# Gate and up projections: hi and lo of the tokens in one matmul of 512 columns

## The chip, the cores and the metric

One core of one Trainium2 chip runs the whole program. The metric is the device time of one execution in microseconds (us): the median of three runs. All numbers of where the time goes come from one profiled execution of the same kernel, whose times are counted from the first instruction.

## What is computed

Three decoder layers on 256 tokens of 1024 features, in f32. Each has a mixer (a first kind in layer 1, another in layers 2 and 3), an out-projection, and a feed-forward part. The change is in the feed-forward part, which is the same in all three layers:

```python
h = rms_norm(x, gain)                                   # [256, 1024]
f = (jax.nn.silu(h @ w_gate) * (h @ w_up)) @ w_down     # 1024 -> 2816 -> 1024
x = x + f                                               # in layer 1: x + rms_norm(f, gain)
```

## The kernel before, in words

**Hi and lo.** Products run in fp32r. For precision each side of a product is a pair: hi, the value rounded to fp32r, and lo, what is left. `h @ w` is made of three products: hi by hi, lo by hi, hi by lo. A weight tile of 128 x 1024 (512 KB) comes by one DMA into `wraw` (3 buffers, `raw_weight`, L267 to L270). `split` (L276 to L284) makes `whi` from it on ScalarE (ACT, L279) and `wlo` on VectorE (DVE, L281); each has 5 buffers. `wraw` is free again when L281 is done, and then the next DMA can start, so the three `wraw` buffers go round in a ring: DMA, ACT, DVE, DMA.

**The feed-forward part** (`ffn`, L528 to L602) walks over 22 tiles `f` of 128 hidden features. Tiles 0 and 1 are made with tokens on partitions, ahead of the loop (L556 to L575). The loop (L577 to L595) takes f = 2 to 21. For each `f`, gate and up are made one after the other by `fm` (L427 to L433), with features on partitions and all 256 tokens as the columns that pass the array: for each of the 8 k-tiles three matmuls of 256 columns, L431 (`whi` by hi of the tokens), L432 (`whi` by lo of the tokens), L433 (`wlo` by hi of the tokens). That is 48 matmuls of 256 columns for each `f`. Gate fills the first half of a PSUM bank and up the second; even tiles use a bank of tag `p`, odd ones of tag `r`, two banks each.

The bank is then read: ACT makes silu of the gate half (L583), DVE multiplies it by the up half (L584), ACT makes hi of the hidden tile (L586) and DVE lo (L587). The tiles `sl` and `hd` share 10 buffers of one tag. The hidden tile passes the down projection (`flush`, `down`, `rows`, `mm3`: L313 to L315, matmuls of 512 columns into the banks `s`, `t`, `o`) one turn later, behind gate and up of the next `f`.

The last six tiles (NLATE) go into the result of tokens 0 to 127 in the loop, and into that of tokens 128 to 255 only behind it (L599 to L601), so that the next norm can begin on the first half of the tokens. Their down weights are split into space of the mixers (`weight_to`, L291 and L292), with no need of a `whi` buffer. The weights of the next layer's in-projection follow in the same ring of `wraw`.

**The tokens.** `put_T` (L382) writes hi (ACT, L389) and lo (DVE, L390) of the normed rows into two tiles, `hTh` and `hTl`, each 8 k-tiles by 256 tokens. The latent attention of layers 2 and 3 uses their space again (`room`, L1394).

**The order of the work.** Each engine runs its instructions in order, in the order that the framework's scheduler gives them when the program is built, by its own estimate of durations; it starts from the order of the program text. So an ACT or DVE instruction that waits for a matmul holds back what stands behind it on its engine, the splits of weights among them.

Of the kernel before, what the change touches and what calls it, by code (L numbers as in the profile page):

```python
# [10 lines left out]
F32 = mybir.dt.float32  # L11
F32R = mybir.dt.float32r
# [6 lines left out]
S = 256  # L19
# [8 lines left out]
# columns of "pcol" (parameters that go with features on partitions)  # L28
# [15 lines left out]
# rows of "prow" (parameters that are spread over all partitions)  # L44
# [11 lines left out]
# constants: the arrays they come in, name and number of columns  # L56
# [8 lines left out]
# Slots of a tag are given out in order: streams that run side by side have tags of their own.  # L65
# [6 lines left out]
class Names:  # L72
    """what the parts of a mixer share"""


# the order in which the steps of a layer's mixers are laid down. Layer 1: (b)ias, (p)rojections, attention of
# the first (m) and the last (n) heads, linear (r)ecurrence, (g)ated linear attention. Layers 2 and 3: (i)nverses,
# (v)alues, (o)perands and outp(u)ts of the recurrence, the rest of the (c)ompressed inputs, (d)ilated and (l)atent attention.
PLAN1 = "pprpbbrppmmpgbmgpmgrgbgprprggngngppngnr"
PLAN2 = "iciiiiiididlilliviiliiiolloodooilioidooidiilolodouullioouuuouluu"  # L80
# the order of the feature tiles in the out-projections
# [12 lines left out]
def _consts():  # L94
# [29 lines left out]
    # column j is distance j - 127  # L124
# [12 lines left out]
def _tm(k, *cols):  # L137
    return [(i, i + k, *cols) for i in range(0, KC, k)]


def _fm(*starts):
# [3 lines left out]
# weight tiles [128, k-tiles, columns] of the in-projections, in the order of their use  # L145
G1 = (_tm(2, 2320, 2576, 768, 1024) + _fm(1296, 1424, 1808, 1936)   # mv of four heads | gv, mq, mk of four heads
      + _fm(0, 128, 512, 640) + _tm(2, 2576, 2832, 1024, 1040)      # lru_x, gq, gk, mv | g_lr
      + _fm(1552, 1680, 2064, 2192) + _tm(4, 1040, 1296)            # mq, mk, g_out
      + _fm(256, 384))                                              # lru_g
G2 = (_tm(2, 1824, 2272, 1024, 1056) + _tm(4, 1568, 1824)              # cq | ckv | krope | lora input, dilated v  # L150
      + _fm(768, 896, 256, 384, 0, 128, 512, 640)                      # lora inputs, k, r, v
      + _tm(2, 1056, 1568))                                            # dilated q | k
# [16 lines left out]
def _pack_ffn(gate, up, down):  # L169
    g = np.asarray(gate).reshape(KC, 128, FC, 128)  # L170
    u = np.asarray(up).reshape(KC, 128, FC, 128)
    d = np.asarray(down).reshape(FC, 128, D)
    # the first two tiles of features: k-tiles in pairs, columns (gate | up)
    h = np.stack([g[:, :, :2], u[:, :, :2]], 2).reshape(4, 2, 128, 512).transpose(0, 2, 1, 3).reshape(4, 128, 1024)
    g, u = (v.transpose(2, 1, 0, 3).reshape(FC, 128, 1024) for v in (g, u))
    rest = np.stack([g[2:], u[2:], d[2:]], 1).reshape(-1, 128, 1024)
    return np.ascontiguousarray(np.concatenate([h, d[:2], rest], 0))
# [6 lines left out]
def layout(i):  # L184
    """The arrays of the launch: the inputs, laid out anew."""
# [46 lines left out]
def tile_kernel(ctx: ExitStack, tc: tile.TileContext, a: dict, out: bass.AP, taps: dict = {}):  # L232
# [33 lines left out]
    # ---------------------------------------------------------------- weights  # L266
# [5 lines left out]
    def weight(ap, E=None):  # L272
        """the pair (hi, lo) whose sum is ap [128, n]"""
        return split(raw_weight(ap), E)
# [11 lines left out]
    def weight_to(ap, his, los):  # L286
        """the same, in tiles that are given: lists of pieces along the columns"""
# [23 lines left out]
    def mm3(o, xs, ws, start, stop):  # L311
        """o += x^T w for the pairs (hi, lo) of both sides, but for lo times lo."""
# [4 lines left out]
    # ---------------------------------------------------------------- start  # L317
# [38 lines left out]
    # ---------------------------------------------------------------- norms  # L356
    @contextmanager
    def behind(done):
        """what is laid down inside is issued after the instructions done"""
# [12 lines left out]
    def mean_rstd(src0, src1, eps_n=1.0 / 32):  # L372
        """1 / rms of the rows [src0, src1] of 2 x 512 columns"""
# [8 lines left out]
    def put_T(src, n, dst, k0, t, tag):  # L382
        """n blocks [128 tokens, 128] of src to dst (hi, lo)[:, k0 + i, tokens of tile t]"""
# [9 lines left out]
    def norm(t, g, add=None, late=False):  # L393
        """the normed rows of tile t, in halves; add(h) first makes half h of x; late: g comes late"""
# [19 lines left out]
    def rows_T(xs, t, dst, tags="rr"):  # L414
        """features on partitions"""
# [10 lines left out]

    def fm(wt, hT, o):  # L427
        """128 features (the columns of the tile wt), all tokens: o [128, 256]"""
# [6 lines left out]
    def tm(wts, hT, t, o):  # L435
        """tokens of tile t on partitions; wts: tiles along k"""
# [10 lines left out]
    # ---------------------------------------------------------------- attention  # L447
    def softmax_head(sp, bias, scale, vs, o):
        """sp: bank with the scores [128, 128 | 256] of both query tiles; bias [128, 256]; vs: v of the two key
        tiles; o [features, 256 tokens]: the result"""  # L450
# [19 lines left out]
    def attention(score, bias, scale, v, h0, nh, dh, mixT, k0):  # L470
        """heads h0 .. h0 + nh - 1: their outputs are the feature tiles of mixT from k0 on. score(h, bank) puts
        the scores, v(h) are the values of both key tiles."""
# [14 lines left out]
    # ---------------------------------------------------------------- out-projection and feed-forward  # L487
# [3 lines left out]
    def rows(acc, t, xs, w, first, last):  # L491
        """both halves of tile t: acc += xs^T w"""
# [3 lines left out]
    def more_room(j):  # L496
        """tiles for a pair (hi, lo) of [128, 2 x 512], in space that the mixers use"""
# [5 lines left out]
    def out_proj(ap, mixT, order, acc, nlate, room=()):  # L503
        """the last nlate k-tiles go into the result of tile 0 before that of tile 1; room: tiles for the first of them"""
# [23 lines left out]
    def ffn(ap, hT, norm):  # L528
        """norm(t) makes the rows of tile t in hT; returns the two halves of the result for tile 0, then those for tile 1. The first two tiles of 128 hidden
        features are made with tokens on partitions, one tile of tokens after the other; the last NLATE go into  # L530
        the result of tile 0 before that of tile 1."""
# [45 lines left out]
        for f in range(2, FC):  # L577
            p = bank("pr"[f % 2])
            for i in range(2):
                w = weight(ap[3 * f + i])  # L580
                fm([v.rearrange("p (k c) -> p k c", k=KC) for v in w], hT, p[:, i * 256:(i + 1) * 256])
            sl = A2("sl", [128, 2, S])
            n_.silu = A.activation(sl[:, 0], p[:, :256], AF.Silu)  # L583
            V.tensor_mul(sl[:, 1], sl[:, 0], p[:, 256:])  # L584
            hd = A2("hd", [128, 2, S], F32R)
            A.activation(hd[:, 0], sl[:, 1], AF.Copy)  # L586
# [11 lines left out]
        # one half after the other: what follows begins with the first  # L598
# [25 lines left out]
    def lay(plan, **streams):  # L624
        """lays down the steps of the streams in the order that their letters have in plan, then what is left"""
# [6 lines left out]
    def proj2(W, i, hT):  # L632
        """two tiles of 128 features: one bank"""
# [14 lines left out]
    # ================================================================ layer 1  # L648
    def layer1():
        hT = pairT("hT")  # L650
# [15 lines left out]
        # the rows of tile 0 go ahead of the rest  # L666
# [12 lines left out]
        # distance bias: row p of a tile begins one column later than row p - 1; the last key is the first column  # L679
# [21 lines left out]
        # projections  # L701
        def inputs():
# [37 lines left out]
            for t in range(2):  # L740
                p = bank("p")[:, :256]
                tm(wg, hT, t, p)
                gate = n.vg[t][:, 256:]             # x / (1 + e^-x), with the table of the attention
# [11 lines left out]
        # attention with distance bias  # L755
# [11 lines left out]
        # gated linear recurrence  # L767
        def lru():
# [3 lines left out]
            # -8 softplus(-lambda), right for small values too  # L772
# [3 lines left out]
            A.activation(sp[0], sp[0], AF.Exp, scale=-1.0)            # z = e^-|lambda|  # L776
            A.activation(sp[1], sp[0], AF.Ln, bias=1.0)               # y
            A.activation(sp[2], sp[1], AF.Exp)                        # e^y
            A.activation(sp[3], sp[1], AF.Tanh, scale=0.5)
            V.scalar_tensor_tensor(sp[3], sp[2], 1.0, sp[3], op0=ALU.add, op1=ALU.mult)   # e^y - 1  # L780
# [33 lines left out]
            V.scalar_tensor_tensor(th, rr, 1.0, th, op0=ALU.add, op1=ALU.mult)   # a^2 - 1  # L814
# [13 lines left out]
        # gated linear attention  # L828
# [77 lines left out]
        hT = pairT("hT")  # L906
# [4 lines left out]
    # ================================================================ layers 2 and 3  # L911
    rope = {}

    def rope_tables():
        """cos, sin [128 tokens, 2 tiles, 8 + 32]"""
# [31 lines left out]
    def rotate(dst, src, nh, r, t, j0):  # L947
        """dst, src [128, nh, 2 r]: halves of r turned by the angles from j0 on"""
# [11 lines left out]
    def solve(LN, Nd, Z, X):  # L960
        """LN[head] [s, chunk, (-L^T | .), t]; Z [s, chunk and head, t]: the transposed inverse of I + L; Nd [s, chunk and head, t]: the blocks
        of 32 on the diagonals of -L^T; X is room for the inverse of its first 64 rows"""
# [6 lines left out]
        # the blocks of 32 on the diagonal, side by side: Zd [s, chunk and head, t], Xd their transposes  # L969
# [24 lines left out]
        # blocks of 64  # L994
# [22 lines left out]
        # of 128  # L1017
# [12 lines left out]
    def latent_in(l, W, hT, norm):  # L1030
        """C, the last inputs of the gate (last() gives them, features on partitions) and the dilated values"""
# [57 lines left out]
    def recurrent(l, W, hT, mixT, last):  # L1089
        """parts that go on side by side: up to the inverses, what else the outputs are made of, the outputs"""  # L1090
# [420 lines left out]
```

## Time and profile before

| what | us |
|---|---|
| median of three runs | 1029.22 |
| lowest and highest of them | 1025.89, 1037.37 |
| span of the profiled execution, first to last instruction | 1023.1 |
| median less that span | 6.1 |
| TensorE matmul (PE) busy | 981.7 (96%) |
| VectorE (DVE) busy | 602.8 (59%) |
| ScalarE (ACT) busy | 514.3 (50%) |

Of the profiled execution itself only the span is told; what lies around it is taken as the difference from the median. PE is TensorE's matmuls and PEld its weight loads, which overlap them. Matmuls overlap each other too: the time from the start of one to the start of the next is what each costs in a row of them, not the duration that is shown for one.

### The profile page before, as it was taken

To read this page: it belongs to the slowest core of one execution; us is meant where nothing else is said; L and a number is where in the kernel's file an instruction comes from. 1 tells how busy PE (TensorE), PEld (TensorE's weight loads), DVE (VectorE), ACT (ScalarE), POOL (GpSimd) and SP (SyncE) were. 2 spreads that over 40 slices of the span, in tenths; PEclk is the share of its full clock that TensorE was granted. 3 is DMA by queue.
4 is the path that set the end of the run, shared out by engine and by line. 5 is a ranking of instruction groups with operands and counts; after the bars stand their busy time and mean duration, and the time that the engine had idled before them with its cause. 6 is when DMAs were issued, how large, how long until landed. Compare 5 with 4: busy or idle time off the path is not lost.

```text
span 1023.1 us, 18418 instructions
## 1 busy us (share of the span) xinstructions
PE 981.7 (96%) x7463; PEld 869.5 (85%) x7463; DVE 602.8 (59%) x1079; ACT 514.3 (50%) x890; POOL 132.3 (13%) x136
## 2 busy tenths in 40 slices
PE   6999989999999998999999999999899999999997
PEld 4988769999997977787899999889678879999996
DVE  5777565555666676455555456566854475555553
ACT  6378564444555554355544445457245464444542
POOL 0004320000001144115000000010441320000000
PEclk9999999999999999999999999999999999999999
DMA  8762446555675415105566667624321246555651
GB/s 256 257 197 89 158 164 205 185 186 185 210 236 154 152 53 151 49 27 163 183 190 185 185 186 230 198 97 157 96 82 42 74 146 198 186 186 188 214 170 41
DMA packets 48641, 161.45 MB, mean 158 GB/s; under 512 B 5683, under 2 KB 9004, under 8 KB 48556
## 3 DMA queue, kind: packets, MB, share of 16 engines
q1 hardware_dynamic: 48556, 160.28, 49.5%
q8 instruction: 58, 0.95, 0.4%
q14 instruction: 27, 0.22, 0.1%
HBM read 159.20 MB, written 1.06 MB: 157 GB/s over the span
## 4 chain that ended last, share of the span: by engine, by line
PE 72%; DVE 9%; DMA 8%; ACT 4%; issue 3%; POOL 3%; SPq 0%; POOLq 0%; ACTq 0%
PE psp L433 7%; PE psp L431 7%; PE psp L432 7%; DMA wraw<-in_ffn_dram 5%; PE psr L433 5%; PE psr L432 5%; PE psr L431 5%; ACT whi L279 3%; PE pss L313 3%; PE pss L314 3%; PE pss L315 3%; DMA wraw<-in_win_dram 2%; DVE wlo L281 2%; PE psp L442 2%; PE psp L443 2%
## 5 line engine op out<-in xcount | busy, mean ns | idle before, releaser
L279 ACT ACTIVATE whi<-wraw 128x1024 fp32r<-128x1024 f32 (+3 forms) x266 | 276.0, 1040 | 315.0 <-PE psp L432 61.9
L281 DVE TENSOR_TENSOR wlo<-wraw,whi 128x1024 fp32r<-128x1024 f32 (+2 forms) x230 | 282.2, 1229 | 241.8 <-ACT whi L279 240.6
L431 PE MATMUL psp<-hTh,whi 128*128 128x256 f32 x720 | 205.1, 285 | 0.0
L433 PE MATMUL psp<-hTh,wlo 128*128 128x256 f32 x720 | 204.5, 284 | 0.0
L432 PE MATMUL psp<-hTl,whi 128*128 128x256 f32 x720 | 204.3, 284 | 0.0
L431 PEld LDWEIGHTS psp<-hTh,whi 128*128 128x128 f32 x720 | 137.8, 191 | 4.0 <-issue 1.7
L432 PEld LDWEIGHTS psp<-hTl,whi 128*128 128x128 f32 x720 | 137.9, 192 | 1.5 <-issue 0.2
L433 PEld LDWEIGHTS psp<-hTh,wlo 128*128 128x128 f32 x720 | 137.9, 192 | 1.2 <-issue 0.3
L432 PE MATMUL psr<-hTl,whi 128*128 128x256 f32 x480 | 135.8, 283 | 0.0
L433 PE MATMUL psr<-hTh,wlo 128*128 128x256 f32 x480 | 135.8, 283 | 0.0
L431 PE MATMUL psr<-hTh,whi 128*128 128x256 f32 x480 | 135.7, 283 | 0.0
L283 POOL TENSOR_TENSOR wlo<-wraw,whi 128x1024 fp32r<-128x1024 f32 (+1 forms) x36 | 80.5, 2247 | 103.9 <-ACT whi L279 99.6
L431 PEld LDWEIGHTS psr<-hTh,whi 128*128 128x128 f32 x480 | 92.0, 192 | 1.2
L432 PEld LDWEIGHTS psr<-hTl,whi 128*128 128x128 f32 x480 | 92.0, 192 | 1.1
L433 PEld LDWEIGHTS psr<-hTh,wlo 128*128 128x128 f32 x480 | 92.0, 192 | 0.0
L367 POOL TENSOR_TENSOR rstd<-msq,neghalf 128x1 f32<-128x1 f32 x18 | 13.3, 737 | 594.7 <-DVE msq L379 594.7
L442 PE MATMUL psp<-whi,hTh 128*128 128x512 f32 (+2 forms) x128 | 48.3, 385 | 3.7 <-ACT hTh L389 3.1
L443 PE MATMUL psp<-wlo,hTh 128*128 128x512 f32 (+2 forms) x128 | 47.1, 376 | 0.0
L586 ACT ACTIVATE hd<-sl 128x256 fp32r<-128x256 f32 x60 | 24.4, 407 | 20.4 <-DVE sl L584 20.4
L442 PEld LDWEIGHTS psp<-whi,hTh 128*128 128x128 f32 x128 | 24.6, 192 | 10.5 <-ACT hTh L389 5.1
L315 PE MATMUL pss<-wlo,hd 128*128 128x512 f32 x84 | 33.3, 397 | 0.0
L314 PE MATMUL pss<-whi,hd 128*128 128x512 f32 x84 | 33.1, 394 | 0.0
(627 smaller groups left out, 1780.0 us busy)
## 6 DMA issues: line engine op xcount, KB each, us to landing
wraw<-in_ffn_dram SPq DMA_DIRECT2D x198, 512.0 KB, 3.9
wraw<-in_win_dram SPq DMA_DIRECT2D x48, 512.0 KB, 4.1
wraw<-in_wout_dram SPq DMA_DIRECT2D x24, 512.0 KB, 3.7
gain<-in_prow_dram SPq DMA_DIRECT2D x9, 512.0 KB, 4.6
wraw<-in_win_dram SPq DMA_DIRECT2D x8, 480.0 KB, 4.0
wraw<-in_win_dram SPq DMA_DIRECT2D x4, 272.0 KB, 3.4
tb<-bdr SPq DMA_DIRECT2D x4, 256.0 KB, 3.8
wraw<-in_wuq_dram SPq DMA_DIRECT2D x2, 512.0 KB, 3.7
```

Of the source, the lines that this page charges most:

```text
L279: A.activation(hi, raw, AF.Copy)
L281: V.tensor_sub(lo, raw, hi)
L283: E.tensor_tensor(lo, raw, hi, op=ALU.subtract)
L313: PE.matmul(o, xs[0], ws[0], start=start, stop=False)
L314: PE.matmul(o, xs[1], ws[0], start=False, stop=False)
L315: PE.matmul(o, xs[0], ws[1], start=False, stop=stop)
L431: PE.matmul(o, wh, hT[0][:, k, :], start=(k == 0), stop=False)
L432: PE.matmul(o, wh, hT[1][:, k, :], start=False, stop=False)
L433: PE.matmul(o, wl, hT[0][:, k, :], start=False, stop=(k == KC - 1))
L442: PE.matmul(o, hT[0][:, k, ts], ws[k][0], start=k == 0, stop=False)
L443: PE.matmul(o, hT[0][:, k, ts], ws[k][1], start=False, stop=False)
L586: A.activation(hd[:, 0], sl[:, 1], AF.Copy)
```

## The change

The pair of the tokens becomes one tile `[128, KC, 2, S]`, hi and lo side by side for each k-tile; the views hi and lo of it are used as before, and `room` takes its space as one tile. For f = 2 to 20 a new `fm_wide` sends hi and lo of a k-tile through the array behind one load of `whi`, as one matmul of 512 columns into a whole bank, and then the hi half alone behind `wlo`, into the second half of that bank. Gate takes a bank of tag `p`, up one of tag `r`. The sum of the two halves is made when the bank is read: ACT copies the second half into a new tile `cr`, DVE adds the first half. Silu and the product then read `cr`. `cr` shares the 10 buffers of `sl` and `hd`. Tile 21 stays as it was, in a bank of tag `p`. Comments of the program text are taken out; they do nothing.

```diff
+    def inputT():
+        t = big.tile([128, KC, 2, S], F32R, name="hT", tag="hT")
+        return t[:, :, 0], t[:, :, 1], t
+
+    def fm_wide(wt, hT, o):
+        for k in range(KC):
+            PE.matmul(o, wt[0][:, k], hT[2][:, k], start=(k == 0), stop=False)
+            PE.matmul(o[:, S:], wt[1][:, k], hT[0][:, k, :], start=False, stop=(k == KC - 1))
...
         for f in range(2, FC):
-            p = bank("pr"[f % 2])
-            for i in range(2):
-                w = weight(ap[3 * f + i])
-                fm([v.rearrange("p (k c) -> p k c", k=KC) for v in w], hT, p[:, i * 256:(i + 1) * 256])
             sl = A2("sl", [128, 2, S])
-            n_.silu = A.activation(sl[:, 0], p[:, :256], AF.Silu)
-            V.tensor_mul(sl[:, 1], sl[:, 0], p[:, 256:])
             hd = A2("hd", [128, 2, S], F32R)
+            if f < FC - 1:
+                cr = A2("cr", [128, 2, S])
+                for i in range(2):
+                    p = bank("pr"[i])
+                    w = weight(ap[3 * f + i])
+                    fm_wide([v.rearrange("p (k c) -> p k c", k=KC) for v in w], hT, p)
+                    A.activation(cr[:, i], p[:, S:], AF.Copy)
+                    V.tensor_tensor(cr[:, i], p[:, :S], cr[:, i], op=ALU.add)
+                    if i == 0:
+                        n_.silu = A.activation(sl[:, 0], cr[:, 0], AF.Silu)
+                V.tensor_mul(sl[:, 1], sl[:, 0], cr[:, 1])
+            else:
+                p = bank("p")
+                for i in range(2):
+                    w = weight(ap[3 * f + i])
+                    fm([v.rearrange("p (k c) -> p k c", k=KC) for v in w], hT, p[:, i * 256:(i + 1) * 256])
+                n_.silu = A.activation(sl[:, 0], p[:, :256], AF.Silu)
+                V.tensor_mul(sl[:, 1], sl[:, 0], p[:, 256:])
             A.activation(hd[:, 0], sl[:, 1], AF.Copy)
...
-        room = [big.tile([128, 4, 512], F32, name=n, tag=n) for n in ("hTh", "hTl")]
-        room = [v[:, i] for v in room for i in range(4)]
+        room = big.tile([128, KC, 512], F32, name="room", tag="hT")
+        room = [room[:, i] for i in range(KC)]
...
-        hT = pairT("hT")
+        hT = inputT()
```

The last replacement stands four times: for the in-projections and for the feed-forward part, in `layer1` and in `layer2`.

## Rows read from the trace of the kernel before

**Rows 1.** Page, busy time of each engine over the span

```profile
PE 981.7 (96%) x7463; PEld 869.5 (85%) x7463; DVE 602.8 (59%) x1079; ACT 514.3 (50%) x890; POOL 132.3 (13%) x136
```

**Rows 2.** Busy time of each engine by stage (us, busy and count, then clock, DMA)

```profile
152.00:260.00 108.00, 108.00 (x762) 101.47 (x762) 55.72 (x64) 47.87 (x63) 0.00 (x0) 1.00 0.58 189
614.00:646.00 32.00, 31.78 (x232) 30.03 (x231) 18.78 (x25) 16.37 (x24) 0.00 (x0) 1.00 0.76 230
850.00:1004.00 154.00, 154.00 (x1108) 145.53 (x1107) 80.46 (x99) 69.13 (x98) 0.00 (x0) 1.00 0.56 183
```

**Rows 3.** Timeline of all engines in the first feed-forward part (start, duration)

```profile
200.65 0.37 ACT L583 ACTIVATE sl<-psr 128x256 f32<-128x256 f32 x1
...
202.10 0.39 PE L315 MATMUL pso<-wlo,hd 128*128 128x512 f32 x1
...
202.33 0.28 PE L431 MATMUL psp<-hTh,whi 128*128 128x256 f32 x1
...
204.54 0.42 DVE L587 TENSOR_TENSOR hd<-sl,hd 128x256 fp32r<-128x256 f32 x1
...
207.96 0.28 PE L433 MATMUL psp<-hTh,wlo 128*128 128x256 f32 x1
...
208.08 0.39 PE L313 MATMUL pss<-whi,hd 128*128 128x512 f32 x1
...
210.63 0.39 PE L315 MATMUL pso<-wlo,hd 128*128 128x512 f32 x1
```

**Rows 4.** Timeline of PE, head tiles with the tokens as stationary side

```profile
136.36 0.39 PE L442 MATMUL psp<-whi,hTh 128*128 128x512 f32 x1
...
137.95 0.39 PE L443 MATMUL psp<-wlo,hTh 128*128 128x512 f32 x1
```

**Rows 5.** Groups by line and form: busy us, mean ns, then idle before

```profile
L584 DVE TENSOR_TENSOR sl<-sl,psr 128x256 f32<-128x256 f32 x30 | 12.4, 414 | 6.5 <-ACT sl L583 6.5
...
L583 ACT ACTIVATE sl<-psp 128x256 f32<-128x256 f32 x30 | 11.1, 368 | 4.5 <-PE psp L433 4.5
```

**Rows 6.** Chain that ended last, end of the first feed-forward part

```profile
264.33 3.68 DMA wraw<-in_ffn_dram
...
290.83 4.14 DMA wraw<-in_ffn_dram
295.08 1.07 ACT whi L279
296.17 1.22 DVE wlo L281
297.42 4.11 DMA wraw<-in_win_dram
...
303.84 0.34 DVE sl L584
...
314.11 3.60 DMA wraw<-in_win_dram
317.89 0.87 issue
318.76 0.68 ACT junk L377 x2
```

**Rows 7.** Timeline of DVE, then of PE, at the same boundary

```profile
316.15 1.38 DVE L615 TENSOR_TENSOR pg<-pss,gain 128x512 f32<-128x512 f32 x2 [0.82 <-PE pss L315]
...
326.57 1.20 PE L386 MATMUL psr<-c,xs 128*128 128x128 f32 x8 [1.69 <-DVE xs L410]
```

**Rows 8.** Chain that ended last, end of the second feed-forward part

```profile
616.86 4.76 DMA wraw<-in_ffn_dram
...
637.75 6.23 DMA wraw<-in_ffn_dram
...
646.76 0.42 ACT hd L586
```

**Rows 9.** Timeline of PE behind those rows

```profile
647.23 0.50 PE L313 MATMUL pss<-AR,hd 128*128 128x512 f32 x1 [1.45 <-ACT hd L586]
```

More of the change, by code (lines that the diff above doesn't have):

```diff
@@ L72 @@
 class Names:
+    pass
 PLAN1 = "pprpbbrppmmpgbmgpmgrgbgprprggngngppngnr"
@@ L905, in layer1 @@
         g2 = gain("pre_ffn")
-        hT = pairT("hT")
+        hT = inputT()
         res = ffn(a["ffn1"], hT, lambda t: normT(t, g2, hT, add_normed(acc, t, g1), "ss"))
@@ L1453, in layer2 @@
     def layer2(l, g, add):
-        hT = pairT("hT")
+        hT = inputT()
         mixT = pairT("mixT")
@@ L1464, in layer2 @@
         out_proj(a[f"wout2_{l}"], mixT, [int(k) for k in ORDER2], acc, 3)
-        hT = pairT("hT")
+        hT = inputT()
         res = ffn(a[f"ffn2_{l}"], hT, lambda t: normT(t, g2, hT, add_plain(acc, t)))
```

## The prediction

> **What bounds the kernel now.** I read the profile's page first. PE is busy 96% of the span and no other engine over 59% [rows 1], so the question is whether PE's own pace sets the end, stage by stage. [...] The timeline then gives PE's pace there [rows 3]: from the first matmul of gate and up (202.33) to the last (207.96) are 47 steps, 5.63 / 47 = 119.8 ns each; then 12 matmuls of 512 columns for the down projection, 11 steps from 208.08 to 210.63, 231.8 ns each. A tile f takes 48 x 119.8 + 12 x 231.8 ns = 8.53 us.
>
> PE full is not the same as PE deciding, so I read the chain of waits last. In the third feed-forward part it runs along PE. At the end of the first it does not [rows 6]: from 264.33 it goes round the ring of weight buffers, DMA 4.14, ACT 1.07, DVE 1.22, next DMA (one turn about 6.6 us); eight DMA rows of that kind stand in it, the last at 314.11. Its last split of a weight goes to ACT, and the squares of the next norm (318.76) stand behind that split, though the result they read was there at 316.15, when DVE took it up [rows 7]. PE then sits idle 1.69 us for that norm [rows 7]. At the end of the second part four such DMA rows stand in the chain, and PE waits 1.45 us for a hidden tile, with a late weight (6.23 us of DMA) ahead of it in the chain [rows 8, 9]. So in these two places the weights set the end, and PE only before them.
>
> **The change part by part.**
> *Matmuls.* For each k-tile three steps of 119.8 ns (359.4) become one of 512 columns and one of 256. The trace has no wide matmul of this form; its nearest rows are the down projection, 231.8 ns, and the head tiles, where the same tokens and gate and up weights meet with sides exchanged: 7 steps from 136.36 to 137.95, 227.1 ns [rows 4]. The step from a 512 matmul to a 256 one is seen once for each f, 0.23 us (202.10 to 202.33), the other way 0.12 (207.96 to 208.08) [rows 3]: changing sizes costs nothing of its own. So a k-tile costs 346.9 to 351.6 ns, which saves 12.5 or 7.8; by 16 k-tiles (gate and up) 0.20 or 0.125 us for each f. I take 0.20, from the head tiles, since the operands are the same. The saving is only the part of a matmul that does not grow with its columns; the columns that pass the array are as many as before. With 19 tiles in each of three layers, 57 x 0.20 = 11.4 us leave PE (7.1 at the lower bound).
>
> [...]
>
> *Reading the banks.* Each f gets two ACT copies of 128x256 out of PSUM and two DVE additions. Rows of that size are 368 ns (silu) and 414 ns (product) [rows 5]: 0.74 us of ACT and 0.83 of DVE for each f. In the loop's middle they are hidden: DVE is busy 55.72 of 108 us and ACT 47.87 [rows 2], that is 4.4 and 3.8 of 8.53 us, so they come to 5.2 and 4.5. The way of the hidden tile grows by one addition, since gate is copied, added and put through silu while up passes PE (2.9 us for 1.15 us of work). Before, that way takes 4.31 us, from 200.65 to 204.96, and the down projection asks for the tile at 208.08 [rows 3]: 3.1 us are spare, against 0.41, or 1.64 if a weight's lo of 1.22 [rows 6] gets in between. Silu and product now read SBUF; the ACT rows of that shape differ by some 0.03 us, nothing here. Were the cover gone, each f would cost up to 0.74 + 0.83 = 1.57 us.
>
> *What is queued behind the new waits.* A copy that waits for PE holds the weight splits behind it on ACT, and an addition those on DVE; behind them wait the next DMA of the ring and, later, PE. In the middle the ring is ahead and waits for PE. At the end of the first two loops it is the chain, and each turn passes ACT and DVE. Below, nothing is added: silu, product and the two of the hidden tile, four instructions of the same length, lie in that stretch already, and only one product of 0.34 us shows in the chain [rows 6], with one 0.42 us in the second part [rows 8]. Above, all four new ones lie in each of the 8 + 4 turns: 12 x 1.57 = 18.8 us. I take 1.0 us at each of the two ends, somewhat over the 0.34 and 0.42 that the existing four leave there, as theirs are placed well by luck or not.
>
> *Banks, buffers, one tile for the pair.* Gate and up have two banks each, used again two tiles later, when they have long been read. `cr` is a third tile for each f in the 10 buffers: six `hd` of the late tiles, and `sl`, `cr` of two tiles are 10 at the worst, by count enough. The joint tile of hi and lo is written and read through the same views. Nothing for these three.
>
> *The sum.* The ring leaves PE at 264.33 in the first part; by then (264.33 - 152) / 8.53 = 13 tiles are done. Up to there what PE saves starts the ring earlier: 13 x 0.20 = 2.6 us. What PE saves behind it is lost, since the ring keeps its pace and PE only waits longer. The second part has the same shape: 2.6. In the third the chain is PE: 19 x 0.20 = 3.8. Together 9.0, less 2 x 1.0 for the ring: 7.0 us. The span of 1023.1 becomes 1016.1. The median of the runs shown lies 6.1 above the span, and I leave that: 1029.2 - 7.0 = **1022.2 us**, 0.7% faster.
>
> **The rivals.**
> *Slower: the ring slips.* Place: the ends of the first two loops, ACT and DVE queues. If copies stand ahead of splits and wait for PE, each turn of the ring grows. It decides from 9.0 / 12 = 0.75 us for each turn; with all 1.57 the balance is +9.8, 1039 us. For it: the ring is in the chain, and copies add waits for PE to ACT. Against it: in that stretch ACT and DVE are idle over a third of the time, and the four instructions there already cost the chain almost nothing.
> *No saving: a wide matmul takes as long as two narrow ones, 239.6 ns.* Then only the ring's 2.0 us are left, 1031 us. For it: the trace has no such matmul into a bank whose second half the next one adds to. Against it: both rows of 512 columns. [...]
> *All of it and more: the ring lets go.* If the splits at the boundaries fall behind the norm's squares, PE decides everywhere: 3.8 in each part, plus the 1.69 us that PE idles in the first boundary: 13.1 us, 1016 us. For it: the order there is the scheduler's and is made anew, and the squares lost 2.6 us (316.15 to 318.76) by it. Against it: the DMAs at these ends take as long as before, 3.60 to 6.23 us [rows 6, 8].
>
> **How the numbers follow.** Forecast 0.55, with 1018 to 1028 as its own range (PE's saving at 0.125 gives 45 x 0.125 - 2.0 = 3.6 us, 1025.6; the ring for nothing 9.0, 1020.2; 2 us on either side for scatter); the ring slips 0.13; no saving 0.12; the ring lets go 0.20. The three executions shown spread by 1.1%, and about 1% is what a measurement of this kernel can tell from no change. Faster by over 1% is below 1018.9: nearly all of the last case and the fast edge of the forecast, 0.25. Slower by over 1% is above 1039.5: the heavy half of the slipping ring, 0.08. Within 1%: 0.67. The range 1013 to 1035 leaves out the heavy half of the slip and an order of the boundaries better than I see.
>
> **What would show it.** Right: the wide line at steps of about 0.23 us and the narrow at 0.12, one f in 8.33 us in the loop, PE without gaps there; the third feed-forward part 3.8 us shorter, the first two 1.5 to 2 us; PE's idle time at the two boundaries longer than 1.69 and 1.45 us. Wrong: wide steps near 0.24; gaps of PE inside the loops that end at a hidden tile or a weight split; the third part shorter by another amount than the loop's 19 tiles; or boundaries where the norm's squares no longer stand behind a split.

## The result and the profile after

The changed kernel takes 1038.93 us (median of 20 runs, 1025.44 to 1057.96), the kernel before 1030.06 us beside it (20 runs, 1021.61 to 1042.77): a ratio of 1.0071, 95% interval 1.0043 to 1.0099. (Ratios leave out the slow runs, those over 1.5% above the fastest of their kernel, so none here is exactly the quotient of two medians.) I had forecast 1022.2 us. The profiled execution has a span of 1032.0 us for 1023.1, at a mean granted clock of 0.980 for 0.995. Each profile is one execution; how much executions differ is told with the experiments.

Cut at the first and last matmul of each stage (a feed-forward part is the stretch of its down projections, a mixer runs from there to the first matmul of its out-projection), the 8.9 us are

| stage | before | after | difference |
|---|---|---|---|
| start to out-projection 1 | 104.94 | 106.20 | +1.26 |
| feed-forward 1 | 176.26 | 175.23 | -1.02 |
| mixers of layer 2 | 128.66 | 137.94 | +9.29 |
| feed-forward 2 | 178.38 | 173.72 | -4.66 |
| mixers of layer 3 | 125.51 | 132.30 | +6.79 |
| feed-forward 3 | 176.33 | 173.11 | -3.23 |

and +0.4 in all that lies between. The stage that was changed gave 8.9 us. The two mixers, in which no line of arithmetic was changed, took 16.1.

First the part that was changed. The timeline of PE, for the same tile f as [rows 3]:

```profile
202.36 0.40 PE L315 MATMUL pso<-wlo,hd 128*128 128x512 f32 x1
202.60 0.40 PE L436 MATMUL psp<-hT,whi 128*128 128x512 f32 x1
202.83 0.28 PE L437 MATMUL psp<-hT,wlo 128*128 128x256 f32 x1
202.95 0.39 PE L436 MATMUL psp<-hT,whi 128*128 128x512 f32 x1
...
208.03 0.28 PE L437 MATMUL psr<-hT,wlo 128*128 128x256 f32 x1
208.15 0.39 PE L313 MATMUL pss<-whi,hd 128*128 128x512 f32 x1
```

Gate and up of one f take 208.15 - 202.60 = 5.55 us, 346.9 ns for a k-tile. In [rows 3] it was 208.08 - 202.33 = 5.75: 0.20 us less. The stretches that answer to [rows 2] show that nothing waits there:

```profile
152.00:260.00 108.00, 108.00 (x568) 92.01 (x567) 67.45 (x91) 58.10 (x92) 0.00 (x0) 1.00 0.61 194
...
860.00:1010.00 150.00, 150.00 (x803) 128.56 (x802) 97.23 (x138) 82.91 (x138) 0.00 (x0) 1.00 0.61 190
```

PE is busy 108.00 of 108.00 us as before, now with DVE 67.45 for 55.72 and ACT 58.10 for 47.87: 11.7 and 10.2 us of copies and additions that lie beside PE.

The page shows where to look for the loss. Its row of the granted clock had only nines before; now two places drop:

```profile
PE 986.5 (96%) x6551; PEld 829.6 (80%) x6551; DVE 652.3 (63%) x1193; ACT 552.1 (53%) x1004; POOL 132.4 (13%) x136
...
PEclk9999999999999999889999999999988999999999
```

912 matmuls fewer [rows 1], and PE is busy 4.8 us longer. The busy time by stretch of the mixers of layers 2 and 3 (columns: stretch, length, then PE, PEld, DVE, ACT and POOL busy with counts, clock, DMA share, GB/s), after:

```profile
404.40:431.70 27.30, 27.09 (x523) 21.06 (x524) 13.73 (x35) 12.26 (x28) 6.84 (x6) 0.94 0.22 69
431.70:448.80 17.10, 17.10 (x101) 14.11 (x98) 4.09 (x14) 3.99 (x9) 0.88 (x1) 0.50 0.01 2
448.80:462.00 13.20, 13.20 (x99) 11.38 (x98) 6.79 (x30) 7.50 (x23) 1.48 (x1) 1.00 0.15 51
769.60:779.90 10.30, 10.30 (x158) 8.58 (x143) 4.33 (x11) 2.10 (x4) 0.49 (x2) 0.50 0.01 2
```

and before, at the first of these places and over most of the mixers of layer 3:

```profile
431.70:448.80 17.10, 17.06 (x148) 14.57 (x147) 8.83 (x36) 10.20 (x29) 2.36 (x1) 1.00 0.13 39
755.00:798.00 43.00, 42.85 (x478) 35.51 (x478) 22.30 (x71) 20.16 (x54) 6.83 (x6) 1.00 0.09 32
```

The clock column is the point: 0.50 for 17.1 us in layer 2 and for 10.3 in layer 3, where before has 1.00. PE is busy in every one of these microseconds as far as the profile shows, and does about half as much in them: eight matmuls of L1291 take 1.90 us there (from 433.26 to the next start at 435.16), and 0.93 ahead of the stretch (428.40 to 429.33). By that, an estimate, up to (17.1 + 10.3) / 2 = 13.7 us are lost. (Both profiles have 3.4 us more at half clock in the mixers of each of the two layers; they cancel.) What PE works on there, from its groups in 431.7 to 448.8 us:

```profile
L1291 PE MATMUL psp<-vc,MN 128*128 128x64 f32 x16 | 3.8, 418 | 0.0
L1243 PE MATMUL psp<-AR,ka 64*128 64x256 f32 x4 | 2.1, 671 | 0.0
L1045 PE MATMUL psr<-X,LN 64*64 64x64 f32 x16 | 2.0, 314 | 0.0
L1050 PE MATMUL psr<-Z,v 64*64 64x64 f32 x16 | 2.0, 314 | 0.0
```

Short matmuls, many of them on 64 rows of the array, and on 32x32 pieces of it just before; nothing of the recurrence or the attention is new.

The rest of the loss is a wait. The timeline of all engines in front of it, layer 2:

```profile
399.69 1.13 POOL L1423 MEMSET room<- 64x512 f32 x2
...
400.47 2.75 DVE L472 TENSOR_SCALAR sc<-sc,rc 128x128 f32<-128x128 f32 x1
...
400.80 2.33 POOL L283 TENSOR_TENSOR wlo<-wraw,whi 128x1024 fp32r<-128x1024 f32 x1
403.14 0.34 DVE L473 TENSOR_SCALAR sc<-sc,rc 128x256 f32<-128x256 f32 x1
403.40 0.85 DVE L1436 COPY room<-pst 64x256 f32<-64x256 f32 x2
404.30 0.25 PEld L1434 LDWEIGHTS pst<-c,qrt 128*128 128x128 f32 x2 [4.46 <-DVE room L1436]
404.30 0.65 PE L1434 MATMUL pst<-c,qrt 128*128 128x128 f32 x2 [4.06 <-DVE room L1436]
```

and before, the same transposes and the same scaling:

```profile
401.01 0.44 DVE L460 TENSOR_SCALAR sc<-sc,rc 128x128 f32<-128x128 f32 x1
...
402.40 0.44 PE L1410 MATMUL pst<-c,qrt 128*128 128x128 f32 x2 [1.54 <-DVE hTl L1412]
```

PE waits 4.06 us for 1.54, and the same in layer 3:

```profile
755.43 0.44 PE L1434 MATMUL pst<-c,qrt 128*128 128x128 f32 x2 [4.06 <-DVE room L1436]
```

The scaling of 128x128 that stands ahead of it on VectorE takes 2.75 us for 0.44, and ends (403.22) 0.09 us behind GpSimd's split (403.13). The one ahead of it took 1.84 us and ended (399.72) 0.09 us behind the split ahead (399.63). The long scaling had started 0.33 us before its split, while GpSimd's memset ran. Why VectorE lasts so long beside GpSimd no run shows. Together the two losses are up to 2 x 2.5 + 13.7 = 18.7 us, for 16.1 measured; the waits weigh somewhat less than 2.5 each, since PE's idle time in the two mixers grew by 1.7 and 2.4 us.

Neither is in a line that the change edits. But it gave the pair hi and lo of the tokens one tile, and the latent attention's `room` takes the same place. Set side by side as the two traces have them (matmuls of one line in a row taken as one), TensorE's instructions before and after differ, beside the feed-forward loop, in 19 places of the mixers of layer 2 and the same 19 of layer 3, and first at the transposes whose results go into `room`.

### The profile page after: what moved, and what is told of

Its sections match the earlier page's. It is cut to its first block, busy times and chain, and to the rows that moved or that the text cites. A ratio compares the mean times of both kernels' runs of the same rounds, so it can differ in the third digit from the quotient of the medians.

```text
span 1032.0 us, 16832 instructions
## 1 busy us (share of the span) xinstructions
PE 986.5 (96%) x6551; PEld 829.6 (80%) x6551; DVE 652.3 (63%) x1193; ACT 552.1 (53%) x1004; POOL 132.4 (13%) x136
## 3 DMA queue, kind: packets, MB, share of 16 engines
HBM read 159.20 MB, written 1.06 MB: 155 GB/s over the span
## 4 chain that ended last, share of the span: by engine, by line
PE 76%; DVE 8%; DMA 7%; ACT 3%; issue 3%; POOL 2%; SPq 0%; POOLq 0%; ACTq 0%
PE psp L436 9%; PE psr L436 9%; PE psp L437 5%; PE psr L437 4%; DMA wraw<-in_win_dram 3%; DMA wraw<-in_ffn_dram 3%; PE psp L443 3%; PE psp L445 3%; PE psp L444 3%; PE pss L313 3%; PE pss L314 3%; PE pss L315 3%; PE psp L454 2%; PE psp L455 2%; PE psp L457 2%
## 5 line engine op out<-in xcount | busy, mean ns | idle before, releaser
L279 ACT ACTIVATE whi<-wraw 128x1024 fp32r<-128x1024 f32 (+3 forms) x266 | 275.7, 1039 | 239.2 <-PE psp L436 65.0
L436 PE MATMUL psp<-hT,whi 128*128 128x512 f32 x456 | 162.5, 395 | 0.0
L436 PE MATMUL psr<-hT,whi 128*128 128x512 f32 x456 | 162.2, 395 | 0.0
L437 PE MATMUL psp<-hT,wlo 128*128 128x256 f32 x456 | 128.0, 281 | 0.0
L437 PE MATMUL psr<-hT,wlo 128*128 128x256 f32 x456 | 127.7, 280 | 0.0
L436 PEld LDWEIGHTS psr<-hT,whi 128*128 128x128 f32 x456 | 85.5, 187 | 20.0
L436 PEld LDWEIGHTS psp<-hT,whi 128*128 128x128 f32 x456 | 85.5, 188 | 19.8
L437 PEld LDWEIGHTS psp<-hT,wlo 128*128 128x128 f32 x456 | 86.0, 189 | 3.2 <-DVE wlo L281 0.7
L437 PEld LDWEIGHTS psr<-hT,wlo 128*128 128x128 f32 x456 | 86.2, 189 | 0.0
L443 PE MATMUL psp<-hT,whi 128*128 128x256 f32 x288 | 82.7, 287 | 0.0
L444 PE MATMUL psp<-hT,whi 128*128 128x256 f32 x288 | 82.1, 285 | 0.0
L445 PE MATMUL psp<-hT,wlo 128*128 128x256 f32 x288 | 82.0, 285 | 0.0
L443 PEld LDWEIGHTS psp<-hT,whi 128*128 128x128 f32 x288 | 55.1, 191 | 2.9 <-issue 1.7
L445 PEld LDWEIGHTS psp<-hT,wlo 128*128 128x128 f32 x288 | 55.2, 192 | 0.6 <-issue 0.3
L444 PEld LDWEIGHTS psp<-hT,whi 128*128 128x128 f32 x288 | 55.1, 191 | 0.4 <-issue 0.2
L454 PE MATMUL psp<-whi,hT 128*128 128x512 f32 (+2 forms) x128 | 49.3, 393 | 3.8 <-ACT hT L389 3.4
```

The costliest lines, as they stand in the source:

```text
L279: A.activation(hi, raw, AF.Copy)
L436: PE.matmul(o, wt[0][:, k], hT[2][:, k], start=(k == 0), stop=False)
L437: PE.matmul(o[:, S:], wt[1][:, k], hT[0][:, k, :], start=False, stop=(k == KC - 1))
L443: PE.matmul(o, wh, hT[0][:, k, :], start=(k == 0), stop=False)
L444: PE.matmul(o, wh, hT[1][:, k, :], start=False, stop=False)
L445: PE.matmul(o, wl, hT[0][:, k, :], start=False, stop=(k == KC - 1))
```

## The experiments

Theory J: the joint tile is free at another moment than `hTl` was, by one matmul, and the scheduler, which lays the work by when its inputs and places are ready, made another order of these mixers (no run reads that moment itself). Rival F: the feed-forward's new work does it. Then, under J: is it the wait and the held VectorE (D), or the clock (C)? Each ran beside the kernel before on one chip; the row of before is the one beside e1 to e4 (1032.48 us beside e5 to e8, 1032.83 beside e9 to e11, 1032.64 beside e12, at clocks of 0.987 and 0.988), so rows of different groups are compared by their ratios. The clocks are medians of the runs, the last two columns the difference from the profile of before, for one execution of each kernel.

| run | median us | clock | ratio to before, 95% | mixers 2, 3 | feed-forward, all |
|---|---|---|---|---|---|
| before (23 runs) | 1029.99 | 0.987 | | | |
| after | 1038.93 | 0.976 | 1.0071 (1.0043 to 1.0099) | +9.3, +6.8 | -8.9 |
| e1_merge | 1047.03 | 0.976 | 1.0137 (1.0068 to 1.0206) | +9.5, +15.4 | -1.3 |
| e2_halves | 1029.50 | 0.984 | 0.9959 (0.9917 to 1.0002) | +7.2, +2.9 | -7.3 |
| e3_splits_off_gpsimd | 1031.89 | 0.981 | 1.0002 (0.9965 to 1.0040) | +4.9, +12.3 | -8.1 |
| e4_narrow_reads | 1046.17 | 0.977 | 1.0137 (1.0063 to 1.0210) | +14.0, +15.1 | -0.9 |
| e5_fill | 1031.38 | 0.990 | 1.0003 (0.9960 to 1.0046) | +1.6, +7.6 | -6.0 |
| e6_halves_fill | 1032.49 | 0.992 | 1.0020 (0.9978 to 1.0062) | +2.2, +8.1 | -7.9 |
| e7_halves_splits | 1028.45 | 0.979 | 0.9951 (0.9908 to 0.9994) | +5.5, +0.3 | -6.2 |
| e8_before_fill | 1035.95 | 0.993 | 1.0062 (1.0018 to 1.0105) | +10.6, +3.0 | -0.2 |
| e9_all | 1034.52 | 0.989 | 1.0038 (1.0004 to 1.0073) | +8.3, +6.6 | -7.2 |
| e10_all_256 | 1027.22 | 0.990 | 0.9956 (0.9925 to 0.9986) | +2.3, +0.6 | -6.9 |
| e11_all_4 | 1024.45 | 0.990 | 0.9928 (0.9890 to 0.9965) | +2.7, -0.5 | -6.5 |
| e12_before_extras | 1038.77 | 0.982 | 1.0058 (1.0019 to 1.0097) | -0.8, +14.2 | -1.1 |

Those two columns scatter. TensorE's order in the two mixers is the same in after, e1 and e4, and so is their median clock (0.976 or 0.977), but the one profile of each has 34, 51 and 68 us at half clock there. The profile of before (0.995) lies above the median clock of before (0.987) as well. What a kernel costs is read from its medians; the columns tell where the time went in one execution.

**e1: the joint tile alone.** After, with the loop's old branch for every f:

```diff
-            if f < FC - 1:
+            if f < 0:
...
-                p = bank("p")
+                p = bank("pr"[f % 2])
```

> The joint tile of the tokens (and of the latent attention's room) as in the change, but the gate and up projections as before: three matmuls of 256 columns, one bank. Theory J (the joint tile sets another order of TensorE's work in the mixers of layers 2 and 3, and that costs the time): the three feed-forward stages last what they last before the change (within 1 us each), the second and third mixers are longer by 5 to 10 us each, with the longer wait ahead of the transposes out of c and qrt (about 4 us for 1.5) and with half clock in one or both stretches behind it; the time is that of after plus the 8.9 us that the feed-forward stages gave, 1040 to 1050 us. Rival F (the feed-forward's new work disturbs the mixers, or brings the half clock): the mixers are as before, 1028 to 1032 us.

1047.03 us, as J has it. TensorE's order in the mixers is after's to the instruction, the wait is there, in the timeline of PE:

```profile
410.00 0.44 PE L1434 MATMUL pst<-c,qrt 128*128 128x128 f32 x2 [4.06 <-DVE room L1436]
```

and so is the lower clock, in the busy time by stretch (columns as above):

```profile
424.00:434.20 10.20, 10.20 (x140) 8.53 (x143) 4.25 (x11) 1.77 (x4) 0.52 (x1) 0.50 0.08 26
...
775.50:785.80 10.30, 10.30 (x139) 8.64 (x138) 4.69 (x12) 2.41 (x5) 0.91 (x1) 0.50 0.01 2
792.60:809.70 17.10, 17.10 (x93) 14.18 (x92) 4.30 (x16) 3.99 (x9) 1.41 (x1) 0.50 0.00 1
```

F falls: there is no wide matmul, no copy and no addition in this kernel. There are two misses. The mixers of layer 3 are 15.4 us longer, not 5 to 10, with 34 us at half clock in this execution; and feed-forward 2 is 2.1 us shorter with nothing changed in it, more on that below.

**e2: the tile in halves along k.** The wide matmul needs hi and lo of one k-tile side by side, not all eight k-tiles in one tile. After with

```diff
-        t = big.tile([128, KC, 2, S], F32R, name="hT", tag="hT")
+        t = [big.tile([128, KC // 2, 2, S], F32R, name=f"hT{j}", tag=f"hT{j}") for j in range(2)]
...
-        room = big.tile([128, KC, 512], F32, name="room", tag="hT")
+        room = [big.tile([128, 4, 512], F32, name=f"room{j}", tag=f"hT{j}") for j in (1, 0)]
```

> After, with its joint tile cut in two along the k-tiles (k 0 to 3, k 4 to 7), each with hi and lo; the room of the latent attention takes the two in the order that gives qr and the first inputs the half that the projections leave first. Gate and up projections as in after. Theory J: the mixers' order is again nearly that of before, the second and third mixers are within 3 us of before's, the feed-forward stages are 8.9 us shorter as in after, and the time is 1018 to 1025 us. Rival F: the mixers stay 6 to 9 us longer each, 1034 to 1042 us.

1029.50 us, 9.4 below after with the same wide matmuls. The order of the mixers is nearer to before's (it differs in 11 places of each, where after's differs in 19). J holds in direction; its 1018 to 1025 was missed. In the profile a half clock of 17.1 us stays in the mixers of layer 2 (+7.2), and from before the kernel cannot be told apart (0.9917 to 1.0002).

**e3: no split on GpSimd beside the mixers.** After with

```diff
-                w = halves_of(weight(ap[k], G if i < 6 else None))
+                w = halves_of(weight(ap[k], G if i < 6 and nlate == 5 else None))
```

> After, but the splits of the out-projections' weights of layers 2 and 3 that GpSimd does are done on VectorE. Theory D (VectorE held beside GpSimd's split and memset makes the wait of 4.06 us ahead of the transposes out of c and qrt, and that wait brings the half clock behind it): the two VectorE operations there take 0.44 us instead of 1.84 and 2.75, the wait is 1.5 us or less, no half clock behind it for more than 4 us, mixers 2 and 3 shorter by 5 to 9 us each: 1022 to 1030 us. Rival O (the order of the matmuls is what costs; the held operation is a by-product): the wait falls but the mixers stay within 3 us of after's, 1033 to 1040 us.

1031.89 us, between the two. The same scaling is short again, in the timeline of DVE:

```profile
398.65 0.55 DVE L472 TENSOR_SCALAR sc<-sc,rc 128x128 f32<-128x128 f32 x1
```

The clock is not back, in the busy time by stretch:

```profile
415.00:428.60 13.60, 13.60 (x148) 10.56 (x147) 6.86 (x15) 2.52 (x6) 0.00 (x0) 0.50 0.20 60
776.80:800.60 23.80, 23.80 (x133) 20.12 (x133) 5.73 (x16) 6.44 (x14) 0.00 (x0) 0.50 0.08 23
```

PE's idle time in the two mixers is 5.4 and 5.0 us, under before's 6.8 and 5.6, and the mixers are 4.9 and 12.3 us longer. So the half clock does not need the wait. D is a part, but how large a part stays open: the idle time is 3 us shorter than after's in each of the two, while of the 7 us by medians some 4.7 go with the clock (0.981 for 0.976, at the 9.4 us for 0.01 that a line through after's runs gives). The order of the mixers moved here too, in 25 places of each from after's.

**e4: the new readers without the wide matmul.** After with, behind the first k-tile,

```diff
-            PE.matmul(o, wt[0][:, k], hT[2][:, k], start=(k == 0), stop=False)
+            if k == 0:
+                PE.matmul(o, wt[0][:, k], hT[2][:, k], start=True, stop=False)
+            else:
+                PE.matmul(o[:, :S], wt[0][:, k], hT[0][:, k, :], start=False, stop=False)
+                PE.matmul(o[:, S:], wt[0][:, k], hT[1][:, k, :], start=False, stop=False)
```

> After, but behind the first k-tile the wide matmul is two of 256 columns again: banks, copies and additions as in after, TensorE's work nearly as before. It tells what part of the 8.9 us that the feed-forward stages gave is the wide matmul's, and what the new readers cost. If the wide matmul gives it all (0.18 us per projection, 7 of 8 taken back) the feed-forward stages last 8 us longer than in after plus what the readers cost, up to 1 us a stage: together before's to before's plus 3, and the time 1044 to 1051 us. Rival: half of the gain of the second feed-forward (4.66 us for 2.6 reckoned) was a stall that the new readers or the timing removed; then that stage stays 1.5 to 2 us below before's, and the time is 1042 to 1045 us.

1046.17 us, with e1. Its feed-forward parts stand at +0.8, -1.9 and +0.2 to before, e1's at +0.75, -2.1 and 0.0. Its first k-tile is still wide, which saves 57 x 0.20 / 8 = 1.4 us, so copies and additions cost about 0.4 + 1.4 = 1.8 us in three parts, not the 1.57 for each f of their bare durations. And after lies 1.8, 2.8 and 3.4 us below this run in its three parts: 8.0 us are the wide matmul's, in seven k-tiles of eight.

**e5: work that keeps the array full.** After with, six times in each of the two mixers, a matmul whose result is not used, ahead of the products of L1291 (two) and of the dilated attention's scores (four):

```diff
                     if hh == 0:
                         p = bank("p")
+                        PE.matmul(p, ident, C("scan"), start=True, stop=True)
...
             q, k = qT[h % 2][:, h // 2], kT[:, h // 2]
+            PE.matmul(p, ident, C("scan"), start=True, stop=True)
```

> After, with 12 matmuls added that compute nothing used (six in each of the mixers of layers 2 and 3: the identity against 512 columns, over the full array, into a bank that the next matmul starts anew), placed where the stretch at half clock stands: ahead of the dilated attention's scores and of the products of the value tiles with 64 columns. Each costs about 0.43 us (a 256-column matmul of this type stood 0.21 us after the one before it in after's trace), 5.1 us together. Theory C (most of the loss is the half clock, and it comes because TensorE there works for long on parts of its array): the stretches of 17.07 and 10.24 us at half clock are gone or no longer than 3.4 us each, which gives back up to half of 27.3, 13.6 us: 1029 to 1033 us. Rival (the half clock has another cause, or isn't the loss): 1041 to 1046 us.

1031.38 us, 7.6 us faster than after, clock 0.990. The expectation had the price of the added work wrong. In the trace each of these matmuls of 512 columns in f32 is two rows, 24 for the 12, and the next row starts about 1 us after the first of the two, here at full clock:

```profile
417.18 1.13 PE L1290 MATMUL psp<-c,c 128*128 128x512 f32 x2
418.24 0.24 PE L1000 MATMUL psr<-Xd,LN 32*32 32x32 f32 x2
```

From start to next start the 12 take 11.2 us, not 5.1. The page's clock row, beside after's:

```profile
PEclk9999999999999999999999999999998999999999
```

C's time came, but not all that it named: the long stretch is gone in layer 2, and one of 10.2 us stays in layer 3. Against after's profile the mixers have 23.9 us less at half clock (half of it is 11.9) and 7.8 us less idle time of PE, for 11.2 us of added work: that makes 8.5 us, for 6.9 measured. The added matmuls are laid by the scheduler too, some early (388.88 us), and the long waits went as well, so this run alone does not part C from D.

**e6 and e8: the same added work on e2 and on before.**

> The kernel with the tile cut in halves (the second run of this study, 1029.5 us) with the same 12 added matmuls. Theory C: its half clock of 17.07 us in the second mixer goes, 1029.5 + 5.1 - 8.5, 1022 to 1028 us. Rival: 1033 to 1037 us.

> Before with the same 12 added matmuls. Theory C also says why the runs of before lie between 1024 and 1045 us with clocks of 0.995 to 0.970: with the added work their clock stays above 0.985 and they scatter by less than 10 us, 1027 to 1033 us. Rival: the added 5.1 us on top, 1034 to 1037 us, with the same scatter.

Clocks 0.992 and 0.993, the highest of all, and times of 1032.49 and 1035.95: C's times missed, by 4.5 and 3 us, and e8 still scatters by 14.8 us. The ranges were laid with 5.1 us for the added work, which takes 11.6 and 12.3 us in these traces. It lifts the clock in both; it pays only where more than its own time had been lost. The scatter of before's runs goes with the clock too: 23 of them lie between 1024 and 1045 us at clocks of 0.997 to 0.970, and a line through them gives 8.8 us for 0.01 of the clock; through the 20 of after, 9.4. At one clock (0.985) the two lines stand at 1034.2 and 1029.6: after is the faster program, at a lower clock.

**e7, e9, e10, e11: together.** The halves of e2 and the split of e3; then with the 12 added matmuls (e9), with 12 of 256 columns (e10, below), and with only the first place's four of 512 (e11).

```diff
+                        PE.matmul(p[:, :256], ident, C("scan")[:, :256], start=True, stop=True)
...
+            PE.matmul(p[:, :256], ident, C("scan")[:, :256], start=True, stop=True)
```

> The kernel with the tile in halves, and the splits of the out-projections of layers 2 and 3 on VectorE as in the third run, which took 7 us from after. If the two edits add up (the order of the one, no held VectorE in the other): 1020 to 1025 us. If what each took from after was the same half clock: 1027 to 1032 us.

> The seventh run's kernel (tile in halves, splits on VectorE: 1028.45 us at a median clock of 0.979) with the 12 added matmuls of 512 columns. In the runs of each kernel so far a clock lower by 0.01 goes with 8 to 9.5 us more. Theory C: the clock rises to 0.990 as in the fifth run (from 0.976), which gives back 10 us for 5.1 us of added work: 1021 to 1026 us. Rival (the added work finds no stretch to lift here): 1031 to 1035 us.

> The same with 256 columns in each of the 12 added matmuls, 2.6 us. Theory C with half the work enough: clock 0.988 or more, 1019 to 1024 us. If it isn't enough: clock below 0.983, 1028 to 1032 us.

> The same with only the four added matmuls of 512 columns ahead of the products with 64 columns (two in each mixer), 1.7 us. If the place is what counts and it is this one: clock 0.988 or more, 1018 to 1023 us. If not: clock about 0.980, 1028 to 1032 us.

e7, 1028.45 us, is only 1 us below e2; its waits are gone (4.4 and 3.9 us of idle time) and its clock is 0.979, so the two edits took much the same. e9 was a miss: clock up to 0.989, time up by 6; its added matmuls take 13.6 us in the trace, more than 0.010 of the clock gives back. e10 lands 3 us above its range; its added work takes 6.5 us, not 2.6. e11 is the fastest kernel of the study, 1024.45 us (expected 1018 to 1023), 14.5 below after. With the same waits as e7 (idle 4.4 and 4.1) and four matmuls more (4.9 us in the trace, not 1.7) its clock is 0.990; one stretch of half clock is left in the mixers, the first of these two:

```profile
413.40:423.70 10.30, 10.30 (x103) 7.67 (x106) 3.78 (x11) 0.82 (x3) 0.52 (x1) 0.50 0.09 27
423.70:440.00 16.30, 16.24 (x226) 12.74 (x222) 8.10 (x20) 7.17 (x17) 0.00 (x0) 1.00 0.11 34
```

The intervals of e7, e10 and e11 overlap: that the last 3 or 4 us are the four matmuls' is likely, not shown.

**e12: before with the extras of e11.**

> Before (two tiles, three matmuls of 256 columns) with the same two extras as the eleventh run: splits of the out-projections of layers 2 and 3 on VectorE, four added matmuls. It tells how much of the eleventh run's time is the wide matmul's. If the wide matmul's 8 to 9 us in the feed-forward stages come through once the mixers are in order: 1031 to 1036 us, 7 to 11 us above the eleventh. Rival (the extras alone make it, and the mixers eat the wide matmul's gain whatever they hold): 1023 to 1028 us.

1038.77 us, above both ranges: the extras alone make before slower, by 0.6%, and 14.3 us slower than e11. The feed-forward parts differ by 5.4 us; most of the rest stands in the mixers of layer 3, 14.2 us longer than before's, at half clock in the row of its page,

```profile
PEclk9999999999999999999999999999976999999999
```

and those of layer 2 are 0.8 shorter. The four added matmuls are in this kernel too, and its median clock is 0.982 for before's 0.988: they do not lift it in every order. Each edit near these mixers made another order of them, for good or ill.

## Why the prediction was wrong

**The matmuls: right.** 0.20 us for each f was forecast, 0.20 measured (5.55 for 5.75 us). The wide matmul keeps the head tiles' pace [rows 4]: 0.23 us to the next start (202.60 to 202.83). The 0.20 us are 12.5 ns for each of the 16 matmuls saved.

**Reading the banks: right.** The loop hides it; 1.8 us in all by e4, where I had taken 1.0 at each of two ends.

**The feed-forward parts: near in sum, not each.** Forecast -1.6, -1.6 and -3.8, measured -1.0, -4.7 and -3.2 (-8.9 for -7.0, of which some 2 us in the second part come without the wide matmul too). Against e4, which has everything but the wide matmul, they gave 1.8, 2.8 and 3.4. In the first part the ring still ends it, with the squares behind a weight's split and PE idle for the norm as in [rows 6, 7], and a new wait for a hidden tile. That PE's idle time there would grow was a sign that did not come: 1.63 us for 1.69.

```profile
315.39 0.50 PE L313 MATMUL pss<-dl,hd 128*128 128x512 f32 x1 [0.98 <-ACT hd L610]
...
319.08 0.58 ACT L377 ACTIVATE junk<-pss 128x512 bf16<-128x512 f32 x1
...
326.99 0.41 PE L386 MATMUL psr<-c,xs 128*128 128x128 f32 x2 [1.63 <-DVE xs L410]
```

In the second the wait of 1.45 us [rows 9] is down to 0.41. That term, -1.6 for this part, was mis-sized because I took the stall of the end of this part as fixed. It goes in e1 too, without any wide matmul (that part 2.1 us shorter, no wait above 0.3 us), so it is not the change's saving; why the weights are in time there was not tried.

**"One tile for the pair ... Nothing for these three": the step that failed.** I asked whether the views read the same bytes and whether the buffers suffice, and not who else waits for the place. `room` does, and e1 shows that this edit alone costs more than the whole loss: 1047.03 us, and mixers of +9.5 and +15.4. (Those two are of one execution; after, with the same order, had +9.3 and +6.8.) The price came in two terms that no part of the prediction had. One is a wait of 2.5 us more in each layer, with a VectorE scaling of 2.75 us for 0.44 beside GpSimd's split; without it (e3) the time is 7 us lower, part of that by the clock. The other, the larger in after's profile, is the half clock. The median clock is 0.976 or 0.977 in all three kernels with after's order, 0.984 with the tile in halves, 0.987 before, and with work added over the full array it was higher in six runs, by 0.006 to 0.014 (e5, e6, e8 to e11), not in e12 (0.982 for 0.988). That the joint tile brings the loss is shown, by e1; that it does so by way of the order is argued, from e1, e2 and e4, since no run holds the order fixed. What exactly in an order lets the clock fall was not settled.

**The rivals.** Mine on the slow side had its place in the ring of the loops. The loops were not slower; the rival was right in sign, for a cause that it did not name, and that its 1039 us is the measured time is luck. The ring did not let go either.

**The scatter.** The 1.1% between the three runs shown I took for noise and laid 2 us on either side. It goes with the granted clock (8.8 us for 0.01). Where the clock fell in those runs is not on record; in the profiles none of the fourteen kernels shows a half clock in a feed-forward part, and it stands mostly in these mixers and at the very end. The profile of before has it for 3.4 us in each of them, and I had read no clock outside the feed-forward parts.

## What to carry to other kernels

A tile is a place with a moment at which it comes free. Before joining two, look for every later tile in the same place and compare the built order of the instructions, stage by stage, also where no line was changed; if it moved, the time there is open. Before adding work, read from a trace what one such instruction takes, with all of its rows: here the guess was under half. A joint operand can often be had in smaller tiles (halves along k here), which kept the wide matmul and gave back most of the loss. And read the granted clock in every stage, by run too: where a stage spends part of its time at the half clock, a new order may cost more than the edit gains (here 16.1 us for 8.9).

## What was not expected of the hardware

The granted clock fell to half with PE busy 17.10 of 17.10 us, and for 23.80 of 23.80 in e3, with no wait ahead of it that mattered (27.09 of the 27.30 us ahead of the first were busy). Of the 101 matmuls in the first stretch 77 have 64 columns (16) or take 64x64 (32) or 32x32 (29) of the array. Twelve added matmuls that fill the array raised the median clock from 0.976 to 0.990 in one kernel, and four from 0.979 to 0.990 in another, while in e12 four did not. A VectorE scaling that takes 0.29 us in the median took 2.75, of which GpSimd split a weight for 2.33. And a matmul of 512 columns costs 0.23 us from start to start with fp32r operands, but 1.06 us (417.18 to 418.24 in e5), in two rows of the trace, with the plain f32 operands of the added ones.
